# A log-sum-exp over rows: eighteen loads instead of seventeen, and the store moved from SyncE to ScalarE

## The chip, the cores and the metric

The kernel runs on one core of one Trainium2 chip. A core has TensorE (not used here), VectorE, ScalarE, GpSimd and SyncE, each with its own instruction stream, and 16 DMA engines that carry data between HBM and the on-chip memory (SBUF). The metric is the device time of the program in microseconds, as the median of several executions. A profile is one execution on the chip, recorded instruction by instruction; its span runs from the first to the last instruction of the program and is a little shorter than the measured time.

## The reference

```python
x = np.random.randn(32, 512, 1024).astype(np.float32)     # axis = -1

def reference(x, axis):
    x_max = np.max(x, axis=axis, keepdims=True)
    return (x_max.squeeze(axis)
            + np.log(np.sum(np.exp(x - x_max), axis=axis))).astype(np.float32)
```

The input is 32 x 512 = 16384 vectors of 1024 float32 numbers, 64 MiB (67.1 MB). The output is one number for each vector. The kernel leaves the maximum out: the numbers are drawn from a normal distribution, whose exponentials do not overflow, so it computes log(sum(exp(x))) directly.

## The kernel before

The input is laid out so that partition p holds vectors 128p to 128p+127. One "row" below is one vector on each of the 128 partitions (128 x 4096 B). There are 128 rows. They are loaded in chunks into a ring of 51 rows in SBUF. A chunk is written `(rows, rows summed by VectorE, parts, by halves)`:

```python
CHUNKS = [
    (4, 4, 1, False), (15, 15, 1, False), (16, 16, 2, False), (16, 16, 2, False),
    (16, 15, 2, False), (14, 14, 2, False), (13, 12, 2, False), (9, 8, 1, False),
    (7, 7, 1, True), (5, 4, 1, True), (4, 3, 1, True), (3, 3, 1, False), (2, 2, 1, True),
    (1, 0, 1, False), (1, 0, 1, False), (1, 0, 1, False), (1, 0, 1, False),
]
RING_ROWS = 51
LN_AT = 7      # the first logs are taken ahead of this chunk
LATE = 4       # the last four chunks have sums of their own (in PSUM)
```

Chunks are placed one behind the other in the ring; a chunk that does not fit before the end starts at slot 0 again. A load waits until the last user of its slots, VectorE or ScalarE, is done:

```python
def load(i):
    ...
    if dve_wait:
        nc.sync.wait_ge(dve_done, dve_wait)
    if act_wait:
        nc.sync.wait_ge(act_done, act_wait)
    nc.sync.dma_start(out=ring[:, s : s + r], in_=x_v[:, row : row + r]).then_inc(landed[i], 16)
```

The work on a chunk: ScalarE takes the exponential of the rows in so many parts; VectorE sums each part, either by one reduction over the part, or row by row, adding the two halves of a row and summing as it goes. Rows that VectorE does not sum are summed by ScalarE with the exponential itself (an accumulator).

```python
load(0)
n_early = len(body.instructions)          # what is issued ahead of the opening barrier
nc.scalar.preload_act_table_set("natural_log_exp_and_others")
for i, (r, n_dve, parts, by_halves) in enumerate(CHUNKS):
    if i:
        load(i)
    s, row = place[i]
    if i == LN_AT:
        take_logs(...)                    # logs of the rows before the chunk just done
    if i == len(CHUNKS) - 1:
        take_logs(...)                    # logs of all but the last four rows
    nc.scalar.wait_ge(landed[i], 16)
    for lo, hi in cuts(n_dve, parts):
        nc.scalar.activation(out=ring[...], in_=ring[...], func=Exp).then_inc(act_done, 1)
        nc.vector.wait_ge(act_done, acts)
        if by_halves:
            for j in range(lo, hi):       # half a row plus the other half, with a running sum
                nc.vector.tensor_tensor_reduce(...).then_inc(dve_done, 1)
        else:
            nc.vector.reduce_sum(out=sums[...], in_=ring[...], axis=AX).then_inc(dve_done, 1)
    for j in range(n_dve, r):             # summed by ScalarE itself
        nc.scalar.activation(..., func=Exp, accum_out=total(row + j)).then_inc(act_done, 1)

take_logs(late_row, NB, late[...], dves, acts)          # logs of the last four rows
nc.sync.wait_ge(act_done, acts)
nc.sync.dma_start(out=out_v, in_=res).then_inc(stored, 16)
nc.sync.sem_clear(range(used[0], used[-1] + 1))
```

Behind this the program is rearranged so that the first `n_early` instructions stand ahead of the opening barrier of all engines. A closing barrier of all engines follows the clearing, and after it:

```python
nc.sync.wait_ge(stored, 16)
nc.sync.sem_inc(stored, -16)
```

Of the kernel before, what the change touches and what calls it, by code (L numbers as in the profile page):

```python
# [8 lines left out]


CHUNKS = [
    (4, 4, 1, False), (15, 15, 1, False), (16, 16, 2, False), (16, 16, 2, False),
    (16, 15, 2, False), (14, 14, 2, False), (13, 12, 2, False), (9, 8, 1, False),
    (7, 7, 1, True), (5, 4, 1, True), (4, 3, 1, True), (3, 3, 1, False), (2, 2, 1, True),
    (1, 0, 1, False), (1, 0, 1, False), (1, 0, 1, False), (1, 0, 1, False),
]
RING_ROWS = 51

# [7 lines left out]
@with_exitstack  # L26
def kernel(
    ctx: ExitStack,
    tc: tile.TileContext,
    x: bass.AP,  # L30
    axis: bass.AP,
    out: bass.AP,
):
    nc = tc.nc
    P = nc.NUM_PARTITIONS

    assert axis in (-1, len(x.shape) - 1), f"only last-axis reduction supported, got {axis}"

    x_flat = x.flatten_outer_dims()
    N, D = x_flat.shape  # L40
    assert N % P == 0
    NB = N // P
    assert sum(r for r, *_ in CHUNKS) == NB

    fp32 = mybir.dt.float32
    Exp = mybir.ActivationFunctionType.Exp
    Ln = mybir.ActivationFunctionType.Ln
    Add = mybir.AluOpType.add
    AX = mybir.AxisListType.X

    x_v = x_flat.rearrange("(p t) d -> p t d", p=P)
    out_v = bass.AP(tensor=out.tensor, offset=out.offset, ap=[[NB, P], [1, NB]])

    ring = nc.alloc_sbuf_tensor("ring", [P, RING_ROWS, D], fp32).ap()
    sums = nc.alloc_sbuf_tensor("sums", [P, NB], fp32).ap()
    late = nc.alloc_psum_tensor("late", [P, 512], fp32).ap()
    res = nc.alloc_sbuf_tensor("res", [P, NB], fp32).ap()

    landed = [nc.alloc_semaphore(f"landed{i}") for i in range(len(CHUNKS))]
    act_done = nc.alloc_semaphore("act_done")  # L60
    dve_done = nc.alloc_semaphore("dve_done")
    stored = nc.alloc_semaphore("stored")
    used = sorted(sem.num for sem in [*landed, act_done, dve_done])
    assert used == list(range(used[0], used[0] + len(used)))


    hook = nc.pop_inst_callback()
    symbolic, nc._always_lower_symbolic_ap = nc._always_lower_symbolic_ap, False


    place = []
    row = slot = 0
    for r, *_ in CHUNKS:
        if slot + r > RING_ROWS:
            slot = 0
        place.append((slot, row))
        slot += r
        row += r

    busy = [(0, 0)] * RING_ROWS
    acts = dves = 0

    def cuts(n, parts):
        ends = [-(-n * k // parts) for k in range(parts + 1)]
        return [(lo, hi) for lo, hi in zip(ends, ends[1:]) if lo < hi]

    def load(i):
        (s, row), r = place[i], CHUNKS[i][0]  # L90
        act_wait = max(a for a, _ in busy[s : s + r])
        dve_wait = max(d for _, d in busy[s : s + r])
# [4 lines that stand above are left out]
        nc.sync.dma_start(out=ring[:, s : s + r], in_=x_v[:, row : row + r]).then_inc(  # L97
            landed[i], 16
        )

    def take_logs(lo, hi, src, dve_wait, act_wait):
        nonlocal acts
        nc.scalar.wait_ge(act_done, act_wait)
        nc.scalar.wait_ge(dve_done, dve_wait)
        nc.scalar.activation(out=res[:, lo:hi], in_=src, func=Ln).then_inc(act_done, 1)  # L105
        acts += 1

    late_row = place[-LATE][1]
    assert not any(n_dve for _, n_dve, _, _ in CHUNKS[-LATE:])

    def total(t):
        return late[:, t - late_row : t - late_row + 1] if t >= late_row else sums[:, t : t + 1]

    body = nc.main_func.blocks[-1]
    assert not body.instructions
    load(0)
    n_early = len(body.instructions)

    nc.scalar.preload_act_table_set("natural_log_exp_and_others")  # L119

    logged = 0
    done_before = [(0, 0)]
    for i, (r, n_dve, parts, by_halves) in enumerate(CHUNKS):
        if i:
            load(i)
        s, row = place[i]
        if i == LN_AT:
            logged = place[i - LN_LAG][1]
            take_logs(0, logged, sums[:, :logged], *done_before[i - LN_LAG])
        if i == len(CHUNKS) - 1:  # L130
            take_logs(logged, late_row, sums[:, logged:late_row], *done_before[-LATE])
        nc.scalar.wait_ge(landed[i], 16)
        for lo, hi in cuts(n_dve, parts):
            nc.scalar.activation(  # L134
                out=ring[:, s + lo : s + hi], in_=ring[:, s + lo : s + hi], func=Exp
            ).then_inc(act_done, 1)
            acts += 1
            nc.vector.wait_ge(act_done, acts)
            if by_halves:
                for j in range(lo, hi):  # L140
                    nc.vector.tensor_tensor_reduce(  # L141
                        out=ring[:, s + j, : D // 2],
                        in0=ring[:, s + j, : D // 2],
                        in1=ring[:, s + j, D // 2 :],
                        scale=1.0,
                        scalar=0.0,
                        op0=Add,
                        op1=Add,
                        accum_out=sums[:, row + j : row + j + 1],
                    ).then_inc(dve_done, 1)  # L150
                    dves += 1
                    busy[s + j] = (0, dves)
            else:
                nc.vector.reduce_sum(  # L154
                    out=sums[:, row + lo : row + hi], in_=ring[:, s + lo : s + hi], axis=AX
                ).then_inc(dve_done, 1)
                dves += 1
                for j in range(lo, hi):
                    busy[s + j] = (0, dves)
        for j in range(n_dve, r):  # L160
            nc.scalar.activation(  # L161
                out=ring[:, s + j],
                in_=ring[:, s + j],
                func=Exp,
                accum_out=total(row + j),
            ).then_inc(act_done, 1)
            acts += 1
            busy[s + j] = (acts, 0)
        done_before.append((dves, acts))

    take_logs(late_row, NB, late[:, : NB - late_row], dves, acts)
    nc.sync.wait_ge(act_done, acts)
    nc.sync.dma_start(out=out_v, in_=res).then_inc(stored, 16)


    nc.sync.sem_clear(range(used[0], used[-1] + 1))


    first = nc.main_func.blocks[0]
    head, work = first.instructions, body.instructions  # L180
    end = next(k for k, i in enumerate(head) if i.opcode == "UnconditionalBranch")
    head, tail = head[:end], head[end:]
    for ins in work[:n_early]:
        at = next(
            k for k, i in enumerate(head) if i.engine == ins.engine and i.opcode == "Drain"
        )
        head.insert(at, ins)
    first.instructions = head + work[n_early:] + tail
    body.instructions = []

    nc._always_lower_symbolic_ap = symbolic
    nc.push_inst_callback(hook)


    tc.close()
    tc.compile()
    nc.sync.wait_ge(stored, 16)
    nc.sync.sem_inc(stored, -16)


# [33 lines left out]
```

The softmax here doesn't subtract the row's maximum and nothing guards it: scores larger than these inputs give would overflow.

## Time and profile before

| | us |
|---|---|
| measured time, median of 3 (162.53 to 162.60) | 162.57 |
| span of the profiled execution | 161.2 |
| VectorE busy | 121.0 |
| ScalarE busy | 115.1 |
| reductions on VectorE, 14 of them | 111.2 |
| exponentials on ScalarE without accumulator, 18 of them | 104.4 |
| exponentials with accumulator, 9 of them | 9.3 |
| moved by DMA | 67.18 MB, mean 417 GB/s |

How to read the lines of the profile: a line of the timeline has the start and the duration in microseconds, the engine (DVE is VectorE, ACT is ScalarE, POOL is GpSimd, SPq is SyncE's queue of DMA issues), the line of the kernel, the operation, the output and input by the program's names, the shapes, how often it follows in sequence, and in brackets the idle time of the engine before it and what ended that. The slices divide the span into 40 equal parts; each digit is the busy share in tenths, 9 for 90% or more. The chain of waits follows the work that ended last back to its start. L97 is the issue of a load, L134 the exponential without accumulator, L161 the one with it, L141 the sum by halves, L154 the reduction, L105 the logs, L173 the store.

### The profile page before, as it was taken

The page shows a single profiled execution, that of the slowest core. Times are in us where ns is not written, and L with a number is a line of the kernel's source. Part 1 is how long each engine was busy: PE and PEld are TensorE (multiplying, and loading weights), DVE is VectorE, ACT ScalarE, POOL GpSimd, SP SyncE. Part 2 cuts the span into 40 slices and gives each one's busy share as a digit, 9 for nine tenths or more (in the row PEclk, how much of TensorE's full clock was granted, in tenths as well). Part 3 has the DMA queues.
Part 4 walks back from the last instruction along what each step waited for, and adds up shares of the span by engine and source line. Part 5 has one row for each costly group of instructions (what it writes and reads, how often), then busy time and mean ns, then how long its engine had stood idle before and what let it go on. Part 6 is the DMA issues. An engine that isn't in the chain of part 4 may idle for free.

```text
span 161.2 us, 149 instructions
## 1 busy us (share of the span) xinstructions
DVE 121.0 (75%) x46; ACT 115.1 (71%) x40; POOL 0.2 (0%) x4
## 2 busy tenths in 40 slices
DVE  0028000003999999999999699999999999999892
ACT  3170005996079960999419993999199999999995
POOL 0000000000000000000000000000000000000000
DMA  7999799999999999999979999999899999999991
GB/s 248 516 488 442 320 457 520 390 390 520 390 390 520 390 390 520 390 390 520 407 342 455 455 455 439 423 423 423 376 439 439 427 448 403 432 415 421 410 409 34
DMA packets 2592, 67.18 MB, mean 417 GB/s; under 512 B 288, under 2 KB 416, under 8 KB 928
## 3 DMA queue, kind: packets, MB, share of 16 engines
q1 hardware_dynamic: 2592, 67.18, 97.3%
HBM read 67.11 MB, written 0.07 MB: 417 GB/s over the span
## 4 chain that ended last, share of the span: by engine, by line
DMA 49%; DVE 29%; ACT 20%; issue 0%
DMA ring<-in_x_dram 49%; DVE sums L154 29%; ACT ring L134 17%; ACT ring L161 3%; ACT res L105 0%
## 5 line engine op out<-in xcount | busy, mean ns | idle before, releaser
L154 DVE TENSOR_REDUCE sums<-ring 128x8 f32<-128x8192 f32 (+5 forms) x14 | 111.2, 7994 | 37.1 <-ACT ring L134 37.0
L134 ACT ACTIVATE ring<-ring 128x8192 f32<-128x8192 f32 (+6 forms) x18 | 104.4, 5835 | 43.7 <-DMA ring<-in_x_dram 43.6
L141 DVE CUSTOM_DVE_ANT_0 ring<-ring 128x512 f32<-128x512 f32 x16 | 9.9, 687 | 0.0
L161 ACT ACTIVATE ring<-ring 128x1024 f32<-128x1024 f32 x9 | 9.3, 1041 | 0.0
L119 ACT ACT_TABLE_LOAD x1 | 1.3, 1283 | 0.8 <-PEq L215 0.8
L161 ACT ACTIVATION_READ_ACCUMULATOR ring<-ring 128x1 f32 x9 | 1.6, 173 | 0.0
L141 DVE DVE_READ_ACCUMULATOR2_ANT sums<- 128x1 f32 x16 | 1.3, 83 | 0.0
L105 ACT ACTIVATE res<-sums 128x81 f32<-128x81 f32 (+1 forms) x2 | 0.5, 246 | 0.0
L105 ACT ACTIVATE res<-late 128x4 f32<-128x4 f32 x1 | 0.2, 173 | 0.0
L215 POOL MEMSET const-bfloat16-1.0<- 128x1 bf16 x1 | 0.1, 102 | 0.0
L215 POOL MEMSET const-uint8-127<- 128x1 uint8 x1 | 0.1, 102 | 0.0
L215 POOL MEMSET const-float32-0.0<- 128x1 f32 x1 | 0.1, 99 | 0.2 <-issue 0.2
L215 POOL MEMSET const-float32-1.0<- 128x1 f32 x1 | 0.1, 99 | 0.0
## 6 DMA issues: line engine op xcount, KB each, us to landing
ring<-in_x_dram SPq DMA_DIRECT2D x1, 7680.0 KB, 25.0
ring<-in_x_dram SPq DMA_DIRECT2D x1, 7168.0 KB, 28.6
ring<-in_x_dram SPq DMA_DIRECT2D x1, 6656.0 KB, 35.7
ring<-in_x_dram SPq DMA_DIRECT2D x1, 4608.0 KB, 20.2
ring<-in_x_dram SPq DMA_DIRECT2D x2, 2048.0 KB, 16.2
ring<-in_x_dram SPq DMA_DIRECT2D x1, 3584.0 KB, 28.3
ring<-in_x_dram SPq DMA_DIRECT2D x1, 2560.0 KB, 27.3
ring<-in_x_dram SPq DMA_DIRECT2D x4, 512.0 KB, 27.0
```

The lines of the kernel that those rows point to most:

```text
L105: nc.scalar.activation(out=res[:, lo:hi], in_=src, func=Ln).then_inc(act_done, 1)
L119: nc.scalar.preload_act_table_set("natural_log_exp_and_others")
L134: nc.scalar.activation(out=ring[:, s + lo : s + hi], in_=ring[:, s + lo : s + hi], func=Exp).then_inc(act_done, 1)
L141: nc.vector.tensor_tensor_reduce(out=ring[:, s + j, : D // 2], in0=ring[:, s + j, : D // 2], in1=ring[:, s + j, D // 2 :], scale=1.0, scal ...
L154: nc.vector.reduce_sum(out=sums[:, row + lo : row + hi], in_=ring[:, s + lo : s + hi], axis=AX).then_inc(dve_done, 1)
L161: nc.scalar.activation(out=ring[:, s + j], in_=ring[:, s + j], func=Exp, accum_out=total(row + j),).then_inc(act_done, 1)
L215: nc = _bacc.Bacc("TRN2", target_bir_lowering=False, num_devices=1)
```

## The change

The chunks become eighteen. The first has two rows instead of four, the large ones are somewhat smaller (12 to 15 rows instead of 13 to 16), and towards the end the sizes fall more finely (12, 7, 7, 5, 3, 3, 2 and four single rows). The purpose is to have the first exponential begin sooner and to leave less work behind the last rows. Two loads instead of one are issued ahead of the opening barrier. The store, with the clearing of the semaphores behind it, is issued by ScalarE, which makes the last logs, instead of by SyncE; the wait for the landing of the store goes to GpSimd.

```diff
 CHUNKS = [
-    (4, 4, 1, False), (15, 15, 1, False), (16, 16, 2, False), (16, 16, 2, False),
-    (16, 15, 2, False), (14, 14, 2, False), (13, 12, 2, False), (9, 8, 1, False),
-    (7, 7, 1, True), (5, 4, 1, True), (4, 3, 1, True), (3, 3, 1, False), (2, 2, 1, True),
-    (1, 0, 1, False), (1, 0, 1, False), (1, 0, 1, False), (1, 0, 1, False),
+    (2, 2, 1, False), (14, 14, 1, False), (14, 14, 1, False), (13, 13, 2, False),
+    (15, 15, 2, False), (14, 13, 2, False), (13, 13, 2, False), (12, 9, 2, False),
+    (7, 7, 2, False), (7, 7, 1, True), (5, 4, 1, False), (3, 3, 2, True), (3, 3, 1, True),
+    (2, 2, 1, True), (1, 0, 1, False), (1, 0, 1, False), (1, 0, 1, False), (1, 0, 1, False),
 ]
@@
     load(0)
+    load(1)
     n_early = len(body.instructions)
@@
-        if i:
+        if i > 1:
             load(i)
@@
-    nc.sync.wait_ge(act_done, acts)
-    nc.sync.dma_start(out=out_v, in_=res).then_inc(stored, 16)
-    nc.sync.sem_clear(range(used[0], used[-1] + 1))
+    nc.scalar.wait_ge(act_done, acts)
+    nc.scalar.dma_start(out=out_v, in_=res).then_inc(stored, 16)
+    nc.scalar.sem_clear(range(used[0], used[-1] + 1))
@@
-    nc.sync.wait_ge(stored, 16)
-    nc.sync.sem_inc(stored, -16)
+    nc.gpsimd.wait_ge(stored, 16)
+    nc.gpsimd.sem_inc(stored, -16)
```

## The prediction

> **What bounds the kernel now.** I read the page's slices first, then the chain of waits, then the timeline of ScalarE's starts after a load, and last the timeline of the final microseconds.
>
> ```profile
> span 161.2 us, 149 instructions
> DVE 121.0 (75%) x46; ACT 115.1 (71%) x40; POOL 0.2 (0%) x4
> DMA  7999799999999999999979999999899999999991
> DMA 49%; DVE 29%; ACT 20%; issue 0%
> q1 hardware_dynamic: 2592, 67.18, 97.3%
> ```
>
> The reader is to see that the DMA row is 9 almost from the first slice to the last but one, that the one queue filled 97.3% of the span, and that VectorE and ScalarE are idle a quarter of it. The chain of waits gives VectorE 29%, and this must not be taken for a limit. The chain steps from a load to the instruction that let it be issued, the reduction that freed its ring rows. The load of sixteen rows that waits for the reduction ending at 55.02 us is issued at 55.04 us, while the fourth load of the program, in the queue since 2 us, is still landing: ScalarE gets it at 64.57 us. So 9.5 us of data were queued ahead, and a later issue would have cost nothing. The queue is never empty; the landings show it:
>
> ```profile
> 7.63 3.62 ACT L134 ACTIVATE ring<-ring 128x4096 f32<-128x4096 f32 x1 [5.57 <-DMA ring<-in_x_dram]
> 25.82 13.00 ACT L134 ACTIVATE ring<-ring 128x15360 f32<-128x15360 f32 x1 [14.58 <-DMA ring<-in_x_dram]
> 45.18 13.95 ACT L134 ACTIVATE ring<-ring 128x8192 f32<-128x8192 f32 x2 [6.36 <-DMA ring<-in_x_dram]
> 64.57 13.95 ACT L134 ACTIVATE ring<-ring 128x8192 f32<-128x8192 f32 x2 [5.44 <-DMA ring<-in_x_dram]
> ...
> 116.57 10.54 ACT L134 ACTIVATE ring<-ring 128x6144 f32<-128x6144 f32 x2 [3.49 <-DMA ring<-in_x_dram]
> ...
> 158.28 1.04 ACT L161 ACTIVATE ring<-ring 128x1024 f32<-128x1024 f32 x1
> 159.23 0.15 ACT L161 ACTIVATION_READ_ACCUMULATOR ring<-ring 128x1 f32 x1
> 159.41 0.17 ACT L105 ACTIVATE res<-late 128x4 f32<-128x4 f32 x1
> 159.61 0.35 SPq L173 DMA_DIRECT2D out_dram<-res  x1
> ```
>
> Each start that waited for a load is the time of its landing. 45.18 - 25.82 = 19.36 us is one load of 16 rows; 146.98 - 116.57 = 30.41 us (146.98 is the next ScalarE start that the chain of waits gives to a load) is four loads of 9+7+5+4 = 25 rows. From 16s + f = 19.36 and 25s + 4f = 30.41 come s = 1.206 us for a row and f = 0.066 us for each load besides. A row of all partitions is 128 x 4096 B, so s is 435 GB/s. The first load lands at 7.63 = c + 4s + f, so the constant of the start is c = 2.74 us. The formula puts the last landing at 2.74 + 128 x 1.206 + 17 x 0.066 = 158.23 us; the last exponential starts at 158.28. So the span is 158.23 of DMA at its own pace and then 3.0 us of tail: exponential, sum and log to 159.58, store issued at 159.61 and landed 1.6 us later (the page's DMA issues), which is the end of the span. The measured time is 1.33 us longer than the profiled span (162.53 and 161.2 of the same run).
>
> **What the Trainium skill says.** "DMA: Bandwidth & Descriptors", section "Where 436 GB/s comes from", gives a ceiling of 435.2 GB/s for the way into SBUF; the trace's slope of 435 GB/s sits on it, so no order or size of loads can make the rows come faster, only f and c are left. The same page, section "Issuing engines are not separate DMA queues", says that transfers run on the same 16 DMA engines whichever engine issues them, and that several issuers save only sequencer time; here the trace before has one issuer and neither agrees nor disagrees. Its section "Anatomy of one DMA" puts most of a transfer's fixed cost into the receipt after the last byte; the store here moves 64 KB, at 435 GB/s 0.15 us of its 1.6, so by far most is fixed, which agrees in kind. So I expect the fixed cost of the store to be the same from ScalarE.
>
> **The change part by part.**
>
> *The queue's total.* One load more: + 1 x 0.066. The rows are the same 128. The last landing becomes 2.74 + 154.37 + 18 x 0.066 = 158.30, + 0.07 us.
>
> *First load of two rows, two loads ahead of the barrier.* The first load is issued at 0.00 in both, so c stays. The second was issued at 0.78 us, behind the barrier; now it comes about 0.38 us after the first (the spacing of the issues at 0.78 and 1.16). The queue has 4 rows before (till 7.6 us), two rows after (till 2.74 + 2.41 + 0.07 = 5.2 us), so in both cases the second load is there long before it is needed. Worth 0. The barrier opens some 0.38 us later, and with it the table load of ScalarE (at 0.78 for 1.28 us): 2.5 us, still ahead of the landing at 5.2. Worth 0. What it does is to start VectorE earlier: the second load now has 14 rows and lands at 22.1, not 25.8.
>
> *Ring waits.* The first load that needs freed rows is again the fifth (2+14+14+13 = 43 rows, and 15 more do not fit into 51). It waits for the reduction of 14 rows: landing 22.15, exponential 12.2 us (13.00 for 15 rows, less 0.86), reduction 15.1 us (16.15 less 1.07): issue at about 49.5. The loads queued before it last until 2.74 + 43 x 1.206 + 4 x 0.066 = 54.9. Slack 5.4 us; it was 9.5. Going on in the same way I get for the sixth load 66.4 against 73.0, for the seventh 80 against 90, for the eighth 96.5 against 105.7, more after it. The queue stays full. Worth 0.
>
> *The taper.* Landings by the formula, loads 8 to 18 (12, 7, 7, 5, 3, 3, 2, 1, 1, 1, 1 rows): 120.2, 128.8, 137.3, 143.4, 147.0, 150.7, 153.2, 154.5, 155.8, 157.0, 158.3. ScalarE's steps from start to start: one with accumulation 1.00 us (155.15 to 156.14) or 1.04 ahead of another kind, 2 rows 1.81, 3 rows 2.67, 4 rows 3.5, 5 rows 4.4, 7 rows 6.1. From 120.3: 5, 4 and three single rows end at 131.2; 4+3 rows at 137.4, 0.1 after load 10 landed; 7 rows at 143.4; 4+1 at 148.0, 1.0 behind load 12; 2+1 at 150.75, level with load 13; 3 at 153.4; 2 at 155.2; the single rows start at 155.2, 156.2, 157.2; then the middle log (0.14) at 158.2, and the last row at 158.35. Load 18 lands at 158.30. ScalarE thus comes out level with the last landing, as in the kernel before (158.28 there), and the end moves + 0.07 us with it, not more. VectorE: I get 157.2 for its last half-row sums (687 ns each, 0.615 from start to start), so about 1 us before the middle log needs it; before it ended 0.1 us ahead of it. Neither is worth anything as long as the last landing decides.
>
> *Store on ScalarE.* It removes the hand-over from ScalarE to SyncE, 159.61 - 159.58 = 0.03 us, and puts a wait of ScalarE on its own semaphore in its place, likely the same 0.03. Issue takes 0.35 us on SyncE; the landing counts from its start. I allow + 0.05 for an engine which has issued nothing so far. The clearing and the barrier lie under the 1.6 us of landing: SyncE waited 0.5 us for its own store at the end, so there is room for 0.5 us more. That GpSimd takes the last wait in SyncE's place: 0.
>
> Sum: 0.07 + 0.05 + 0 = + 0.12 us, 162.57 to 162.7 us.
>
> **The rivals.** (1) The earlier second load pays, because the queue starves in the start: for it speaks only the 7 in the first slice, which is the start's latency. It would give 0.4 us, 162.2. Against it: the first load's rows cover it. (2) The finer taper leaves less after the last landing: possible only if ScalarE was late there. It started 0.05 us after the landing, so at most 0.05. In the other direction ScalarE has no slack from load 8 on, and each step that takes 0.1 us longer than I say comes out at the end: up to 163.0. (3) The first transfer from ScalarE's own queue starts slowly. SyncE's first load has c = 2.74 us against 1.4 of fixed cost for the store, which may be a read against a write, or a first use: then up to + 1.3, 163.9. I think a read is the likelier reason. (4) SyncE's early end, or GpSimd as the last engine, changes the 1.33 us outside the span: by some 0.2 either way. (5) The ring waits starve the queue, as the slack falls from 9.5 to 5.4 us: this needs a reduction 5 us slower than the row before shows; nothing speaks for it.
>
> **Range and chances.** Rivals 2 and 4 make the width: 162.3 to 163.1. 2% is 3.25 us, and no rival reaches it: a gain of that size would need the tail and start together to lose more than half of their 5.7 us, a loss of that size a queue that runs dry. Same 0.98, faster 0.01, slower 0.01.
>
> **What would show it.** Right: ScalarE's start after load 2 at about 22.1 us, after load 3 at 39.1, the last exponential at 158.35, the store issued by ScalarE's queue at about 159.7 and landing 1.6 later, DMA row full of nines, VectorE's first long wait shorter. Wrong: a slice of the DMA row below 8 in the middle (ring waits); the last exponential more than 0.2 us after 158.3 (ScalarE bound in the taper); a landing time of the store well over 1.6 (first use); equal spans but unequal times (outside the span).

## The result and the profile after

| | before | changed |
|---|---|---|
| measured time, median of 6 | 162.55 us (162.46 to 162.77) | 163.43 us (163.14 to 163.79) |
| ratio | | 1.0051, 95% interval [1.0036, 1.0066] |
| span of the profiled execution | 161.2 us | 161.0 us |
| mean span of the executions | 161.24 us (50 executions) | 161.28 us (6 executions) |
| measured time minus span, mean | 1.34 us (1.29 to 1.39) | 2.12 us (2.08 to 2.15) |

The changed kernel is 0.5% slower, and its profile does not show it. The last row of the table holds the case: the program between its first and its last instruction takes as long as before, and the time that the measurement has beyond that grew by 0.78 us. (A span is given to 0.1 us, so one difference of time and span is good to 0.05; the means are better.)

The page of the changed kernel: span, busy engines, DMA row of the slices, the two DMA queues that there are now, and the chain.

```profile
span 161.0 us, 153 instructions
DVE 121.5 (75%) x46; ACT 115.3 (72%) x43; POOL 0.2 (0%) x4
DMA  7999999999999969999979999999999999999991
q1 hardware_dynamic: 2592, 67.11, 97.3%
q10 hardware_dynamic: 144, 0.07, 0.1%
DMA 38%; ACT 31%; DVE 28%; issue 1%
```

The reader is to see the same picture: the loads' queue at 97.3% of the span, q10 carrying nothing but the store. The chain has moved 11 points from DMA to ScalarE without any change in what limits the kernel; its shares are not shares of a cost. There is a 6 and a 7 in the middle of the DMA row. The prediction named such a slice as a sign of a starved queue, so the landings on both sides of the 6 (slice 15, 56 to 60 us) decide. The changed kernel's timeline of the first half:

```profile
4.99 1.91 ACT L135 ACTIVATE ring<-ring 128x2048 f32<-128x2048 f32 x1 [2.46 <-DMA ring<-in_x_dram]
...
21.93 12.15 ACT L135 ACTIVATE ring<-ring 128x14336 f32<-128x14336 f32 x1 [15.03 <-DMA ring<-in_x_dram]
...
38.88 12.15 ACT L135 ACTIVATE ring<-ring 128x14336 f32<-128x14336 f32 x1 [4.80 <-DMA ring<-in_x_dram]
49.23 17.28 SPq L97 DMA_DIRECT2D ring<-in_x_dram  x2
...
54.62 11.39 ACT L135 ACTIVATE ring<-ring 128x7168 f32<-128x7168 f32 x2 [3.59 <-DMA ring<-in_x_dram]
72.76 7.03 ACT L135 ACTIVATE ring<-ring 128x8192 f32<-128x8192 f32 x1 [6.75 <-DMA ring<-in_x_dram]
```

From 54.62 to 72.76 fifteen rows land in 18.14 us; the prediction's formula has 15 x 1.206 + 0.066 = 18.16. So the queue did not run dry there, and the 6 cost no time (it is likely only how the records of long transfers fall into slices). The 7 stands in the same slice of the kernel before. The fifth load was issued at 49.23 us, 5.4 us before the queue had landed what was in it.

The end of the changed kernel, from its timeline and its DMA issues:

```profile
156.94 1.05 ACT L162 ACTIVATE ring<-ring 128x1024 f32<-128x1024 f32 x1
157.89 0.17 ACT L162 ACTIVATION_READ_ACCUMULATOR ring<-ring 128x1 f32 x1
157.94 0.25 ACT L105 ACTIVATE res<-sums 128x52 f32<-128x52 f32 x1
158.07 1.06 ACT L162 ACTIVATE ring<-ring 128x1024 f32<-128x1024 f32 x1
159.03 0.17 ACT L162 ACTIVATION_READ_ACCUMULATOR ring<-ring 128x1 f32 x1
159.22 0.17 ACT L105 ACTIVATE res<-late 128x4 f32<-128x4 f32 x1
159.43 0.37 ACTq L174 DMA_DIRECT2D out_dram<-res  x1
```
```profile
out_dram<-res ACTq DMA_DIRECT2D x1, 64.0 KB, 1.6
```

The last exponential starts at 158.07, the store is issued 0.04 us after the last log ends (159.22 + 0.17) and lands 1.6 us later. All of this is what the prediction expected, to 0.3 us. The 0.8 us that were lost are not in it.

### The profile page after: what moved, and what is told of

It is laid out like the page before. It is cut to its first block, busy times and chain, and to the rows that moved or that the text cites. A ratio compares the mean times of both kernels' runs of the same rounds, so it can differ in the third digit from the quotient of the medians.

```text
span 161.0 us, 153 instructions
## 1 busy us (share of the span) xinstructions
DVE 121.5 (75%) x46; ACT 115.3 (72%) x43; POOL 0.2 (0%) x4
## 3 DMA queue, kind: packets, MB, share of 16 engines
q1 hardware_dynamic: 2592, 67.11, 97.3%
## 4 chain that ended last, share of the span: by engine, by line
DMA 38%; ACT 31%; DVE 28%; issue 1%
DMA ring<-in_x_dram 38%; DVE sums L155 28%; ACT ring L135 27%; ACT ring L162 5%; ACT res L105 0%
## 5 line engine op out<-in xcount | busy, mean ns | idle before, releaser
L155 DVE TENSOR_REDUCE sums<-ring 128x7 f32<-128x7168 f32 (+7 forms) x16 | 112.3, 7079 | 35.1 <-ACT ring L135 35.1
L135 ACT ACTIVATE ring<-ring 128x7168 f32<-128x7168 f32 (+8 forms) x21 | 104.6, 5028 | 42.8 <-DMA ring<-in_x_dram 42.8
L142 DVE CUSTOM_DVE_ANT_0 ring<-ring 128x512 f32<-128x512 f32 x15 | 9.3, 687 | 0.3 <-ACT ring L135 0.3
L105 ACT ACTIVATE res<-sums 128x72 f32<-128x72 f32 (+1 forms) x2 | 0.5, 248 | 0.0
```

The costliest lines, as they stand in the source:

```text
L135: nc.scalar.activation(out=ring[:, s + lo : s + hi], in_=ring[:, s + lo : s + hi], func=Exp).then_inc(act_done, 1)
L142: nc.vector.tensor_tensor_reduce(out=ring[:, s + j, : D // 2], in0=ring[:, s + j, : D // 2], in1=ring[:, s + j, D // 2 :], scale=1.0, scal ...
L155: nc.vector.reduce_sum(out=sums[:, row + lo : row + hi], in_=ring[:, s + lo : s + hi], axis=AX).then_inc(dve_done, 1)
```

## The experiments

Each is compared with the kernel before on the same chip (medians of before between 162.27 and 162.68 us). "Outside" is the mean of measured time minus span over all executions of that kernel; for the kernel before it was 1.33 or 1.34 us in every set. The third column counts what the program has more for ScalarE than the kernel before, waits included. (In the traces some waits are part of the instruction behind them: e4 has 5 more there, e11 has 3.)

| run | what differs from the kernel before | ScalarE | ratio [95%] | mean span, before's | outside |
|---|---|---|---|---|---|
| e1 | last wait on GpSimd | 0 | 1.0030 [1.0018, 1.0042] | 161.25, 161.24 | 1.86 |
| e2 | store, clearing on ScalarE | +3 | 0.9996 [0.9990, 1.0003] | 161.22, 161.24 | 1.33 |
| e3 | 18 loads, two early | +4 | 0.9994 [0.9988, 1.0001] | 161.12, 161.24 | 1.34 |
| e4 | e2 and e3 | +7 | 1.0014 [1.0006, 1.0022] | 161.24, 161.24 | 1.56 |
| e5 | last wait on VectorE | 0 | 1.0007 [1.0000, 1.0015] | 161.35, 161.35 | 1.45 |
| e6 | last wait on ScalarE | +2 | 1.0011 [1.0004, 1.0018] | 161.36, 161.35 | 1.49 |
| e7 | one exponential in 9 pieces | +8 | 0.9999 [0.9992, 1.0007] | 161.33, 161.35 | 1.33 |
| e8 | e4, two cuts and a log fewer | +2 | 1.0056 [1.0038, 1.0074] | 162.20, 161.35 | 1.32 |
| e9 | e2 and e7 | +11 | 1.0022 [1.0007, 1.0038] | 161.12, 161.05 | 1.54 |
| e10 | exponentials of 3 loads in pieces | +35 | 1.0013 [1.0001, 1.0025] | 161.21, 161.05 | 1.34 |
| e11 | e4, a log fewer | +4 | 1.0019 [1.0009, 1.0028] | 161.36, 161.05 | 1.33 |
| e12 | last wait on TensorE | 0 | 1.0030 [1.0020, 1.0040] | 161.09, 161.05 | 1.66 |
| e13 | e7, first load by ScalarE | +9 | 1.0003 [0.9993, 1.0014] | 161.22, 161.20 | 1.42 |
| e14 | e2 and e10 | +38 | 1.0011 [0.9999, 1.0024] | 161.42, 161.20 | 1.34 |
| e15 | e3, first load of one row | +4 | 1.0001 [0.9990, 1.0013] | 161.26, 161.20 | 1.35 |
| e16 | changed kernel, a log fewer | +4 | 1.0035 [1.0021, 1.0049] | 161.29, 161.20 | 1.88 |
| e17 | one exponential in 13 pieces | +12 | 1.0002 [0.9994, 1.0011] | 161.29, 161.25 | 1.33 |
| e18 | two exponentials in 18 pieces | +16 | 1.0021 [1.0013, 1.0029] | 161.22, 161.25 | 1.71 |

### The change taken apart: e1 to e4

Theory A: the loss belongs to the engine that ends last. Rivals: the second DMA queue (B), the loads' start (C).

e1, on the kernel before:

```diff
-    nc.sync.wait_ge(stored, 16)
-    nc.sync.sem_inc(stored, -16)
+    nc.gpsimd.wait_ge(stored, 16)
+    nc.gpsimd.sem_inc(stored, -16)
```

> The kernel before with one thing changed: GpSimd, not SyncE, makes the last wait for the store. Theory A (the loss lies behind the span and belongs to the engine that ends last, GpSimd): 163.3 us, with measured time minus span 2.1 us as in the changed kernel, and a span near 161.2. Theory B (a second DMA queue, ScalarE's, costs outside the span): 162.55 us, time minus span 1.35. Theory C (the loads): 162.55 us.

e2, on the kernel before:

```diff
-    nc.sync.wait_ge(act_done, acts)
-    nc.sync.dma_start(out=out_v, in_=res).then_inc(stored, 16)
-    nc.sync.sem_clear(range(used[0], used[-1] + 1))
+    nc.scalar.wait_ge(act_done, acts)
+    nc.scalar.dma_start(out=out_v, in_=res).then_inc(stored, 16)
+    nc.scalar.sem_clear(range(used[0], used[-1] + 1))
```

> The kernel before with the store and the clearing issued by ScalarE, the last wait still on SyncE. Theory A: 162.6 us, time minus span 1.35. Theory B: 163.3 us, time minus span 2.1. Theory C: 162.6 us.

e3 is the new list of chunks with `load(1)` beside `load(0)`, and nothing else of the change.

> The eighteen loads and the two loads ahead of the barrier alone; store, clearing and last wait on SyncE as before. Theories A and B: 162.55 to 162.7 us, the landing of the last load within 0.2 us of the changed kernel's, time minus span 1.35. Theory C (the loads' start costs time ahead of the span): 163.3 us, time minus span 2.1.

e4, on the changed kernel:

```diff
-    nc.gpsimd.wait_ge(stored, 16)
-    nc.gpsimd.sem_inc(stored, -16)
+    nc.sync.wait_ge(stored, 16)
+    nc.sync.sem_inc(stored, -16)
```

> The changed kernel with the last wait given back to SyncE; store and clearing stay on ScalarE. Theory A: 162.65 us, time minus span 1.35. Theory B: 163.4 us as the changed kernel, time minus span 2.1. Theory C: 163.4 us.

e1 says yes to A with 1.86 - 1.34 = 0.52 us, at an unchanged span, where 0.8 had been expected. Its page and its timeline are those of the kernel before, to 0.1 us:

```profile
span 161.1 us, 149 instructions
DVE 121.0 (75%) x46; ACT 115.1 (71%) x40; POOL 0.2 (0%) x4
```
```profile
159.37 0.17 ACT L105 ACTIVATE res<-late 128x4 f32<-128x4 f32 x1
159.56 0.35 SPq L173 DMA_DIRECT2D out_dram<-res  x1
```

What tells them apart is who waits at the end. The waits of SyncE's queue, kernel before:

```profile
SPq L173 <- ACT res L105: 29.1, 1, 29.1
SPq L198 <- SPq L198: 0.5, 1, 0.5
```

L198 is the instruction that waits for the store and lowers its semaphore, and SyncE waits 0.5 us in it. In e1 SyncE's waits have no such line, because GpSimd makes that wait; the span ends right behind the landing all the same.

e2 and e3 clear the store on ScalarE and the loads, taken one by one: neither moves the time nor what is outside. B and C fall in their plain form. But e4, which has both, has 0.22 us more outside, and no theory had that.

### Which engine ends last: e5, e6, e12

The same two lines as in e1, with `nc.vector`, `nc.scalar` and `nc.tensor`.

> The kernel before with the last wait on VectorE. Theory A1 (GpSimd alone ends a program slowly, 1.86 us of measured time behind the span where it waits last, every other engine 1.34): 162.55 us, time minus span 1.34. Theory A2 (SyncE is the one engine that ends quickly, any other adds 0.5): 163.05 us, time minus span 1.86. Theory A3 (each engine has a number of its own, by its place in what follows the program): another value, between 1.0 and 2.2.

> The kernel before with the last wait on ScalarE. Theory A1: 162.55 us, time minus span 1.34. A2: 163.05 us, 1.86. A3: another value, between 1.0 and 2.2.

> The kernel before with the last wait on TensorE. Theory A3 (each engine has a number of its own for the time behind the span; SyncE 1.34, VectorE 1.45, ScalarE 1.49, GpSimd 1.86 so far): a fifth number. Below 1.34 it would be a faster place for the wait; I expect 1.4 to 1.5, 162.65 us.

Five engines, five numbers: 1.34 SyncE, 1.45 VectorE, 1.49 ScalarE, 1.66 TensorE, 1.86 GpSimd, with the spans within 0.05 us of before's. So it is not a fault of GpSimd alone nor a gift of SyncE alone; each engine has its own (A3), and SyncE is the best place for the last wait and GpSimd the worst. TensorE's was expected at 1.4 to 1.5 and came out higher.

The Trainium skill's page "Runtime: NRT & Kernel Launch", section "The ~15µs preamble/postamble breakdown", lists a barrier of all engines and resets of semaphores that follow a kernel. The traces agree. No view prints it, but they keep the updates of semaphores behind the last instruction too: two rounds of nine updates of one semaphore, the first of which may begin just ahead of the last instruction, and in between one update each of some 240 other semaphores, as resets would make them. Counted from the end of the last instruction, in us:

| last wait on | SyncE (before) | VectorE (e5) | ScalarE (e6) | TensorE (e12) | GpSimd (e1) |
|---|---|---|---|---|---|
| first of the other semaphores' updates | 0.25 | 0.32 | 0.36 | 0.53 | 0.74 |
| last update of all | 1.45 | 1.57 | 1.61 | 1.78 | 1.99 |
| time outside the span, same execution | 1.33 | 1.45 | 1.49 | 1.66 | 1.87 |

The last two rows differ by 0.12 us in each column, to 0.01. So what the engine of the last wait costs lies behind the span, most of it ahead of the resets. Why the engines differ is not shown.

### The 0.22 us that neither part has alone: e7 to e11, e13, e14, e16 to e18

What e4 has and e2 and e3 don't is a longer program on ScalarE. e7 makes that program longer and changes nothing else, where ScalarE has idle time:

```diff
-            nc.scalar.activation(
-                out=ring[:, s + lo : s + hi], in_=ring[:, s + lo : s + hi], func=Exp
-            ).then_inc(act_done, 1)
-            acts += 1
+            for a, b in cuts(hi - lo, 9 if i == 1 else 1):
+                nc.scalar.activation(
+                    out=ring[:, s + lo + a : s + lo + b],
+                    in_=ring[:, s + lo + a : s + lo + b],
+                    func=Exp,
+                ).then_inc(act_done, 1)
+                acts += 1
```

> The kernel before with eight more instructions on ScalarE: the exponential of the second load, where ScalarE has time, in nine pieces instead of one. Theory D (the 0.22 us by which loads and store together lengthen the time outside the span, and neither alone, come from the length of ScalarE's program): 162.8 us, time minus span 1.56. Theory E (they come from ScalarE's queue together with the loads ahead of the barrier): 162.55 us, time minus span 1.34.

e8 makes e4's program shorter:

```diff
-LN_AT = 7
+LN_AT = -1
-    (15, 15, 2, False), (14, 13, 2, False), (13, 13, 2, False), (12, 9, 2, False),
+    (15, 15, 2, False), (14, 13, 2, False), (13, 13, 2, False), (12, 9, 1, False),
-    (7, 7, 2, False), (7, 7, 1, True), (5, 4, 1, False), (3, 3, 2, True), (3, 3, 1, True),
+    (7, 7, 2, False), (7, 7, 1, True), (5, 4, 1, False), (3, 3, 1, True), (3, 3, 1, True),
```

> The changed kernel with the last wait on SyncE, and five instructions fewer on ScalarE: two chunks are not cut in two, and the first of the three logs is left out, its rows taken by the second. Theory D: time minus span 1.34, 162.55 to 162.65 us. Theory E: time minus span 1.56, 162.85 us.

The two contradict each other at first: e8 gives the 0.22 us back (1.32), with the loads, the early issue and ScalarE's store all still there, so theory E falls; but e7's longer program does not bring them (1.33), so D falls in its plain form. The span of e8 is 0.9 us longer for a reason of its own, which is plain in its timeline:

```profile
158.23 0.68 DVE L142 CUSTOM_DVE_ANT_0 ring<-ring 128x512 f32<-128x512 f32 x1
158.84 0.08 DVE L142 DVE_READ_ACCUMULATOR2_ANT sums<- 128x1 f32 x1
159.02 0.31 ACT L105 ACTIVATE res<-sums 128x124 f32<-128x124 f32 x1 [0.78 <-DVE sums L142]
159.23 1.04 ACT L162 ACTIVATE ring<-ring 128x1024 f32<-128x1024 f32 x1
```

The middle log waits 0.78 us for VectorE's last sum, and the last exponential starts at 159.23 instead of 158.07 in the changed kernel. Without the cut of the twelve-row load VectorE gets its nine rows in one piece and late, at 128.08 instead of 125.65 us, and never makes it up. e11 below, which leaves out the log alone, has no such wait. By this wait the two cuts together are worth 0.78 us (0.54 if the mean spans of e8 and e11 are compared, each less its before's): VectorE has about 1 us to spare at the end, as the prediction said, and without the cuts this is used up.

e9 joins ScalarE's store (e2) and the pieces (e7), with the seventeen loads of before; e10 has eight pieces for each exponential of the loads 1 to 3, with the store on SyncE; e11 is e4 with `LN_AT = -1` alone.

> The kernel before with the store and the clearing on ScalarE and, besides, eight more instructions there (the second load's exponential in nine pieces). Theory D2 (what follows the program takes 0.22 us longer once ScalarE's program with its DMA issue is longer than that of the short versions; nothing of the loads matters): time minus span 1.56, 162.8 us. Theory F (something of the eighteen loads is needed as well): time minus span 1.34, 162.55 us.

> The kernel before, store on SyncE, with 35 more instructions on ScalarE. Theory D2 in its plain form (length alone): time minus span 1.56 or more, 162.8 us or more. If ScalarE's own DMA queue is needed: 1.34, 162.55 us.

> The changed kernel with the last wait on SyncE and without the first of its three logs (its rows go to the second), which makes ScalarE's program three instructions shorter; the cuts of the chunks stay. Theory D2: time minus span 1.34, span as in the changed kernel plus at most 0.1, 162.6 us. Theory F: 1.56, 162.85 us.

e9 brings the 0.2 us without the new loads (1.54); e11 removes them with three instructions fewer (1.33). So the eighteen loads are not needed, and F falls. e10, the longest program so far, does not have them. Its ratio of 1.0013 comes from its span, as e11's 1.0019 does, 0.16 and 0.31 us above before's. Of e11's, 0.06 us are the middle log, which takes 124 rows instead of 52 and holds up the last exponential by that much more; for the rest I have no shown cause. Spans of the kernel before on that chip lay at 160.8 to 161.0 in 25 of 37 executions and at 161.4 to 161.6 in 6; 10 of e11's 18 lay at 161.4 or above.

Is ScalarE's own DMA queue needed? e13 puts the first load on it, with e7's pieces; e14 joins e2 and e10.

```diff
-        nc.sync.dma_start(out=ring[:, s : s + r], in_=x_v[:, row : row + r]).then_inc(
+        eng = nc.scalar if i == 0 else nc.sync
+        eng.dma_start(out=ring[:, s : s + r], in_=x_v[:, row : row + r]).then_inc(
```

> The kernel before with the first load issued by ScalarE and with eight more instructions there; store and last wait on SyncE. If any use of ScalarE's own DMA queue together with the longer program brings the 0.22 us: time minus span 1.55. If it takes the store at the end: 1.34. In either case the span may be somewhat longer, because the first load now shares the DMA engines with the second.

> The kernel before with store and clearing on ScalarE and 35 more instructions there. If the extra time is a step: time minus span 1.55. If it grows with the length (0.22 us for eight more): about 2.2.

The first two landings in e13's timeline, to which the part on the prediction comes back:

```profile
16.67 3.62 ACT L137 ACTIVATE ring<-ring 128x4096 f32<-128x4096 f32 x1 [14.46 <-DMA ring<-in_x_dram]
...
25.73 4.65 ACT L137 ACTIVATE ring<-ring 128x2048 f32<-128x2048 f32 x3 [5.45 <-DMA ring<-in_x_dram]
```

e13 lies between (1.42); e14, with the store on ScalarE and the longest program of all, is at 1.34 (with a span 0.2 us above before's, for which I have no cause either). So the term neither grows with the length nor is a step in it. The last two runs, both with the store on SyncE, have 12 and 16 instructions more: the second load in 13 pieces; and the first two loads in 4 and 14 pieces.

> The kernel before, store on SyncE, with 12 more instructions on ScalarE. Theory G (a window of program lengths of ScalarE alone brings the 0.2 us, with no DMA issue on it): time minus span 1.55 here or with 16 more. Theory H (a DMA issue on ScalarE is needed as well): 1.34 in both.

> The kernel before, store on SyncE, with 16 more instructions on ScalarE. Theory G: time minus span 1.55 here or with 12 more. Theory H: 1.34 in both.

e18 has 0.37 us more outside (1.71), the most of all, at the same span and without a DMA issue on ScalarE. By its number theory H falls. From the pages of e17 and e18, in this order, span, engines and the exponentials' group:

```profile
span 161.3 us, 161 instructions
DVE 121.0 (75%) x46; ACT 116.2 (72%) x52; POOL 0.2 (0%) x4
L136 ACT ACTIVATE ring<-ring 128x1024 f32<-128x1024 f32 (+6 forms) x30 | 105.5, 3576 | 42.7 <-DMA ring<-in_x_dram 42.6
```
```profile
span 161.2 us, 165 instructions
DVE 121.0 (75%) x46; ACT 116.5 (72%) x56; POOL 0.2 (0%) x4
L136 ACT ACTIVATE ring<-ring 128x1024 f32<-128x1024 f32 (+6 forms) x34 | 105.9, 3176 | 42.3 <-DMA ring<-in_x_dram 42.2
```

Four instructions on ScalarE more (x52, x56), the same span within its spread, and measured medians of 162.68 and 162.93 us. Shown: cutting ScalarE's work into other pieces moves the time outside the span by up to 0.37 us, with no new wait inside it.

But e18's term is not that of e4. The semaphore updates behind the last instruction divide the runs in two. In e18 the last of them comes 1.82 us after the last instruction, 0.37 later than in the kernel before, and in e13 1.54, 0.09 later: their terms lie behind the span. In e4 and e9 it comes at 1.44 and 1.43, as in the kernel before (1.45), and in the changed kernel at 1.99, as in e1. So what these three have more outside (0.23 us in e4's profiled execution, 0.13 in e9's and 0.24 in the changed kernel's, besides GpSimd's share) does not lie there; it must lie ahead of the first instruction or behind the last update, and the traces do not tell which. All three have the store on ScalarE, so for this term theory H does not fall. The store is not enough, however: e2, e8, e11, e14 and e16 have it without the term. By the count of the third column the term comes with +7 and +11 and not with +2, +3, +4 or +38, which a window of lengths would fit as well as anything else in how the program is made up. The rule stays open, and so does whether it is the instructions themselves or where they come to lie in memory.

e16, at last, is the changed kernel with `LN_AT = -1` and GpSimd's wait kept.

> The changed kernel, GpSimd's last wait kept, without the first of its three logs. If the two terms add independently: time minus span 1.86, against 2.12 in the changed kernel. If the 0.22 us there are GpSimd's: 2.12 stays.

1.88 us, e1's number within 0.02. So the changed kernel's 2.12 is GpSimd's 1.86 and another 0.26, which a log and its two waits fewer on ScalarE take away; the two add.

### The size of the first load: e15

```diff
-    (2, 2, 1, False), (14, 14, 1, False), (14, 14, 1, False), (13, 13, 2, False),
+    (1, 1, 1, False), (15, 15, 1, False), (14, 14, 1, False), (13, 13, 2, False),
```

> The eighteen loads and the two early ones, store and wait on SyncE, with a first load of one row and a second of fifteen. If the constant of the start falls with the size of the first load (2.60 us for four rows, about 2.4 for two, over the profiles so far): first landing at about 3.6 us, span 161.05, 162.4 us. If the constant is the same for two rows and one: span as with two rows, 161.12, 162.47 us. Time minus span 1.34 in both.

The first two landings in e15's timeline, and then in e3's:

```profile
3.55 1.06 ACT L135 ACTIVATE ring<-ring 128x1024 f32<-128x1024 f32 x1 [1.02 <-DMA ring<-in_x_dram]
...
22.04 13.00 ACT L135 ACTIVATE ring<-ring 128x15360 f32<-128x15360 f32 x1 [17.43 <-DMA ring<-in_x_dram]
```
```profile
4.82 1.91 ACT L135 ACTIVATE ring<-ring 128x2048 f32<-128x2048 f32 x1 [2.30 <-DMA ring<-in_x_dram]
...
21.73 12.15 ACT L135 ACTIVATE ring<-ring 128x14336 f32<-128x14336 f32 x1 [15.00 <-DMA ring<-in_x_dram]
```

The first landing comes sooner with fewer rows, and the start's constant by the formula is 3.55 - 1.206 - 0.066 = 2.28 us with one row and 4.82 - 2.412 - 0.066 = 2.34 with two in e3. It scatters, though, from one execution to the next: 2.51 to 2.75 in the twelve profiles whose first load has four rows and comes from SyncE (mean 2.62), and 2.19 to 2.70 in the six with two rows (mean 2.41, 2.51 in the changed kernel). The means differ by 0.2 us, and the ranges overlap; with one row there is one profile. The sixteenth row lands at 22.04 with one row first, and between 21.69 and 22.05 in the six with two: nothing is left of the single row's lead. A span of 161.05 had been expected for a gain; it is 161.26, against before's 161.20.

## Why the prediction was wrong

**The bound and the queue's total: right.** The rate held in every load looked at, 16.95 us for fourteen rows from 21.93 to 38.88 by measurement and by the formula.

**The start's constant: mis-sized at most by 0.2 us, without consequence.** "So c stays": it came out 2.51 us, not 2.74, in the profile after, which is within the scatter of profiles with four rows; the means say that it fell by 0.2. The last exponential starts at 158.07, predicted 158.35. Of a gain in span the runs hold nothing: the same loads gave 161.12 against 161.24 in e3, 161.24 against 161.24 in e4, and 161.28 in the changed kernel.

**Two loads ahead of the barrier, the ring waits, the taper: worth 0, right.** The table load moved to 1.25 us and was done before the landing at 4.99. The fifth load's slack was 5.4 us as worked out. ScalarE came level with the last landing; VectorE's slack of 1 us was real, as e8 showed by using it up.

**The store on ScalarE: right within its allowance.** + 0.05 us allowed, e2 measured a ratio of 0.9996 [0.9990, 1.0003]. Rival 3, a slow first use of ScalarE's queue, is refuted by the landing after 1.6 us. (The section "Anatomy of one DMA" of the Trainium skill's page "DMA: Bandwidth & Descriptors", which the prediction quotes, describes a DMA issued by GpSimd; no run here shows where the 1.6 us of this store go.) For loads, e13 agrees with what the prediction quotes from the same page's section "Issuing engines are not separate DMA queues": with the first load on ScalarE's queue and the others on SyncE's, the first lands at 16.67 us instead of 7.63, and the second at 25.73 instead of 25.82. The two queues share one rate.

**The step that failed** is the last one of the sum: "That GpSimd takes the last wait in SyncE's place: 0." It costs 0.52 us (e1), with e16 as the second measurement, and the traces put it behind the last instruction: the last semaphore update comes 1.99 us after it instead of 1.45. I read the last wait as covered by the landing of the store, which it is within the span, and took what lies outside as a constant of 1.33 us. Rival 4 saw that the last engine could change it and gave it 0.2 us either way, with nothing in the profile to size it; the run that would have sized it is e1.

**What no step had** is the 0.26 us that come with ScalarE's longer program (2.12 against 1.88 in e16, 1.56 in e4 against 1.33 in e11). What takes it away is shown, its cause is not. Together: 0.52 + 0.26 outside the span, and 161.28 - 161.24 = 0.04 in it, 0.82 of the measured 163.43 - 162.55 = 0.88 us, which is a difference of medians; that of the means is 0.83. Either of the first two alone would have kept the time at the edge of the range, or within it; both took it past 163.1.

No version beats both kernels. The best is e3, the change's loads with everything at the end left on SyncE: 0.9994 [0.9988, 1.0001] of the kernel before, no difference that the measurement holds, and 0.9 us less than the changed kernel's median.

## What to carry to other kernels

Compare measured time with span before and after: where they part, a view of the span cannot explain the loss, and one-line edits at the program's end may; here they did for the larger part. Leave the last wait of a program with SyncE, unless a measurement on that kernel says otherwise; its place was worth up to 0.5 us here, though the span stayed the same. And a difference of 0.1 or 0.2% that follows from nothing in the span may come from how ScalarE's program happens to be cut: vary that by a few instructions before believing in a cause.

## What the runs showed of the hardware that was not expected

- The engine that makes the last wait sets the time outside the span: 1.34 us SyncE, 1.45 VectorE, 1.49 ScalarE, 1.66 TensorE, 1.86 GpSimd, at equal spans. It does so behind the last instruction, where the last semaphore update comes after 1.45, 1.57, 1.61, 1.78 and 1.99 us.
- The make-up of ScalarE's program changes the time outside the span, not in the order of its length: behind the last instruction by 0.37 us in e18 and 0.09 in e13, and elsewhere, only in kernels with the store on ScalarE, by some 0.2 in e4, e9 and the changed kernel; in e2, e3, e7, e8, e10, e11, e14, e15 and e17 by 0.02 or less.
- Above the rate's share, the first landing came 2.62 us after the start in the mean of twelve profiles with four rows in the first load (2.51 to 2.75), and 2.41 us in the mean of six with two (2.19 to 2.70).
